# A hybrid decoder block: the output projection by seven block products in place of eight

## The chip, the cores and the metric

The kernel runs on one core of a Trainium2 chip. The metric is the device time of one execution in microseconds (us), the median of several runs; lower is better.

## The reference, cut to what matters

One decoder block works on 1024 tokens of width 2048 (with 16 learned tokens ahead of them): a normalisation, an input projection, eight heads of differential attention and a gated linear recurrence (RG-LRU) beside them. Their gated results stand side by side in `mixed`, 1024 features each. Then

```python
mixed = jnp.concatenate([att, rec], axis=-1)
x = x + jnp.einsum('bte,ed->btd', mixed, w_out[l])
return rmsnorm(x, final_g, NORM_EPS)[:, N_META:]
```

The change touches this last part alone: a product of 1024 x 2048 (tokens by features) with 2048 x 2048 (`w_out`), the residual, and the final normalisation, all in float32. `rmsnorm` divides a row by the root of the mean of its squares, so it needs a whole row of the output before it can scale any of it, and multiplies by `final_g`.

## The kernel before, in words

Four kinds of engine take part: TensorE (PE; its weight loads are PEld) multiplies, VectorE (DVE), ScalarE (ACT) and GpSimd (POOL) work element by element. DMAs are issued from SyncE's queue (SP) and from POOL's. Every queue is worked off in order. The code says what is computed; a scheduler sets the order of each queue ahead of time, and `issue_after` ties an instruction behind another one. A tile of a pool with `bufs=n` waits until the n-th tile of its tag before it is free.

Each float32 operand is split into a high part, rounded to the format that TensorE multiplies in, and a low part, the rest (`split`, lines 77 to 80: ScalarE copies `hi`, VectorE subtracts `lo`). A product is three matmuls into one accumulator: high by high, high by low, low by high (lines 643 to 645).

The tokens are worked in two halves of 512 (A and B). The mixed features of half h lie in DRAM as `mix_d[h][e]`, 16 tiles of 128 features by 512 tokens, 256 KB each; e 0 to 7 come from attention, 8 to 15 from the recurrence. `w_out` is stored as tiles `w_out[cg, ep]` of 128 x 1024 (512 KB): column group cg (512 output columns, four of them) and two blocks of 128 features, ep 0 to 7.

`load_w` (line 111) loads such a tile into `wraw` (two buffers) and splits it into `whi` and `wlo` (three buffers each). `load_mix` (line 611) loads and splits a tile of mix.

`out_half` (line 617) is run for half A, then for half B. Its loop goes over the four column groups; in each over eight weight tiles; for each of these over two feature blocks and four blocks of 128 tokens (t), so 24 matmuls of 512 columns to a weight tile. Four PSUM accumulators of a column group take 16 feature blocks each; eight buffers allow the next group to begin. While A is worked, its rows of x are loaded into `y` (four tiles of 128 x 2048) and, in column group 1, the 16 mix tiles of B into a second pool. At the end of a column group, `evacuate` adds each accumulator to `y` on VectorE (line 650), squares it on ScalarE with a running sum (line 651), and on POOL multiplies the first three column groups by `final_g` (line 653). After the fourth, `finish` works out the row's factor (lines 662 to 666), scales the row on ScalarE (L675) and VectorE (L671, L674) and stores it in two DMAs of 512 KB (L677), from POOL's queue for A, from SP's for B.

In the last column group of half B all eight weight tiles are split ahead of time into the buffers that held A's mix tiles (`wlast`), and the loop goes token block by token block, so that a block's end lies beside the matmuls of the next.

Before this stage, the recurrence of half B (lines 797 to 809) uses `hTB` on the right-hand side of SBUF and its own pool on the left.

Of the kernel before, what the change touches and what calls it, by code (L numbers as in the profile page):

```python
# [66 lines left out]
class Trunk:  # L67
# [549 lines left out]
    def out_half(self, half, mix, ypool, next_pool, next_mix, w_pool):  # L617

        nc = self.nc
        ys = []  # L620

        def load_y(t):
            y = ypool.tile([P, D], F32, tag="y", name="y", bufs=4)
            r = half * HALF + t * P
# [4 lines left out]
        def weights(cg, ep):
            if cg < 3 or w_pool is None:  # L630
                (hi, lo), = self.load_w(lambda i: self.w_out[cg, ep], 0, 1)
            else:
                raw = self.wpool.tile([P, 1024], F32, tag="wraw", name="wraw", bufs=2)
                nc.sync.dma_start(out=raw, in_=self.w_out[cg, ep])
                hi, lo = [w_pool.tile([P, 2, HALF], F32R, tag="mix", name="wlast", bufs=16).rearrange("p a b -> p (a b)")
                          for _ in range(2)]
                self.split(hi, lo, raw)
            return [(hi[:, i * 512:(i + 1) * 512], lo[:, i * 512:(i + 1) * 512]) for i in range(2)]

        def product(acc, e, t, w):  # L640
            tk = slice(t * P, (t + 1) * P)
            mh, ml = mix[e][:, 0, tk], mix[e][:, 1, tk]
            nc.tensor.matmul(acc, lhsT=mh, rhs=w[0], start=(e == 0), stop=False)  # L643
            nc.tensor.matmul(acc, lhsT=mh, rhs=w[1], start=False, stop=False)  # L644
            nc.tensor.matmul(acc, lhsT=ml, rhs=w[0], start=False, stop=(e == 15))  # L645

        def evacuate(acc, cg, t):
            y, ss = ys[t]
            c = slice(cg * 512, (cg + 1) * 512)
            nc.vector.tensor_tensor(out=y[:, c], in0=acc, in1=y[:, c], op=ALU.add)  # L650
            nc.scalar.activation(acc, y[:, c], AF.Square, accum_out=ss[:, cg:cg + 1])
            if cg < 3:
                nc.gpsimd.tensor_tensor(out=y[:, c], in0=y[:, c], in1=self.g_b[:, c], op=ALU.mult)
            if cg == 2:
                nc.vector.tensor_reduce(out=ss[:, 4:5], in_=ss[:, 0:3], axis=AX.X, op=ALU.add)
                nc.vector.tensor_scalar(out=ss[:, 4:5], in0=ss[:, 4:5], scalar1=1.0 / D, scalar2=EPS,
                                        op0=ALU.mult, op1=ALU.add)

        def finish(t):
            y, ss = ys[t]  # L660
            r, v, n, m = ss[:, 5:6], ss[:, 3:4], ss[:, 6:7], ss[:, 7:8]
            nc.scalar.activation(r, v, AF.Sqrt, bias=ss[:, 4:5], scale=1.0 / D)
            nc.vector.tensor_scalar(out=v, in0=v, scalar1=1.0 / D, scalar2=ss[:, 4:5], op0=ALU.mult, op1=ALU.add)
# [4 lines left out]
            for q in range(2):  # L668
                c = [slice(1024 * q + 512 * i, 1024 * q + 512 * (i + 1)) for i in range(2)]
# [9 lines left out]
        for cg in range(4):  # L679
            acc = [self.ps.tile([P, 512], F32, tag="o", name="o", bufs=8) for _ in range(4)]  # L680
            if cg == 3 and w_pool is not None:
                ws = sum([weights(cg, ep) for ep in range(8)], [])
                for t in range(4):
                    for e in range(16):
                        product(acc[t], e, t, ws[e])
                    evacuate(acc[t], cg, t)
                    finish(t)
                continue
            for ep in range(8):
                ws = weights(cg, ep)  # L690
                with self.tc.issue_after(self.last_w.ins):
                    if cg == 0 and 3 <= ep < 7:
                        load_y(ep - 3)
                    if cg == 0 and ep == 2 and not half:
                        nc.sync.dma_start(out=self.g_b, in_=self.final_g.partition_broadcast(P))
                        nc.vector.tensor_scalar(out=self.g_b, in0=self.g_b, scalar1=-0.5, scalar2=None, op0=ALU.mult)
                    if cg == 1 and not half:
                        for _ in range(2):
                            next_mix.append(self.load_mix(next_pool, 1, len(next_mix)))
                for i in range(2):  # L700
                    for t in range(4):
                        product(acc[t], 2 * ep + i, t, ws[i])
            for t in range(4):
                evacuate(acc[t], cg, t)
                if cg == 3:
                    finish(t)

    def build(self):
# [11 lines left out]
        self.vm_d = [dram.tile([MR, P], F32, name=f"vm_d{h}") for h in range(H)]  # L720
        self.mix_d = [[dram.tile([P, HALF], F32, name=f"mix_d{x}_{e}") for e in range(16)] for x in range(2)]
# [148 lines left out]
```

## Time and profile before

| | us |
|---|---|
| median of 3 runs | 1667.31 |
| lowest and highest run | 1664.11, 1668.2 |
| the profiled execution, its own time | 1665.55 |
| span of that execution in the trace | 1663.8 |

The profile is a page and a trace of one execution. The page gives the busy time of each engine, the span in 40 slices, and the chain of work that ended last, followed back from the last instruction. The trace can be asked for groups of instructions (by line, engine and tile, with their mean duration and what ended the idle time before them), for an engine's instructions in order of time, for busy time in any stretch, and for the DMAs with their time from issue to landing. A matmul's busy time overlaps that of its neighbours, so its price is the distance between two of them and not its duration. `fg_b` is the tile that holds `final_g`, `o` an accumulator of the output projection.

### The profile page before, as it was taken

How to read it: one execution, taken by the hardware profiler on the slowest of the kernel's cores; microseconds unless marked ns; L12 is line 12 of the kernel's file. 1: busy time of each engine (PE TensorE's matmuls, PEld its weight loads, DVE VectorE, ACT ScalarE, POOL GpSimd, SP SyncE). 2: the span in 40 equal slices, each digit the busy share in tenths (PEclk: the TensorE clock that was granted, in tenths of full speed). 3: DMA queues.
4: the chain of work that ended last, by engine and by line, in shares of the span. 5: the costliest groups of instructions: out<-in, count | busy, mean ns of one | idle time of the engine just before them, and what ended most of it. 6: DMA issues, size and time to landing. Idle time of an engine off the chain costs nothing.

```text
span 1663.8 us, 22995 instructions
## 1 busy us (share of the span) xinstructions
PE 1635.2 (98%) x8658; PEld 1404.3 (84%) x8658; DVE 1013.0 (61%) x2090; ACT 863.5 (52%) x1368; POOL 173.4 (10%) x276
## 2 busy tenths in 40 slices
PE   8999999999999999999999999999999999999997
PEld 6889988999988898888888888887878888888886
DVE  7766556665667667667766866776776553343342
ACT  5655455554475575546555655655875442232232
POOL 1211101111011102001101100000000011111110
PEclk9999999999999999999999999999999999999999
DMA  9633334433344435424323423314433462345332
GB/s 313 200 123 122 112 120 135 132 115 121 112 146 156 131 136 198 116 87 131 124 85 118 130 79 118 107 62 133 143 120 114 179 244 98 99 172 221 101 127 101
DMA packets 68427, 223.85 MB, mean 135 GB/s; under 512 B 9739, under 2 KB 11828, under 8 KB 67164
## 3 DMA queue, kind: packets, MB, share of 16 engines
q1 hardware_dynamic: 46720, 164.91, 29.6%
q0 software_dynamic: 21360, 57.41, 10.9%
q8 instruction: 68, 1.11, 0.3%
q14 instruction: 43, 0.35, 0.1%
q10 hardware_dynamic: 236, 0.06, 0.0%
HBM read 186.09 MB, written 29.37 MB: 130 GB/s over the span
## 4 chain that ended last, share of the span: by engine, by line
PE 89%; issue 3%; DVE 3%; DMA 3%; ACT 2%; POOL 0%; SPq 0%; ACTq 0%; POOLq 0%; DVEq 0%
PE proj L158 19%; PE proj L159 19%; PE proj L160 19%; PE o L645 7%; PE o L644 7%; PE o L643 7%; PE T L396 2%; PE S L341 2%; PE S L339 2%; PE pv L406 1%; PE pv L405 1%; PE pv L407 1%; DMA xraw<-xa 1%; DMA xt<-x 1%; DMA wraw<-w_in 1%
## 5 line engine op out<-in xcount | busy, mean ns | idle before, releaser
L80 DVE TENSOR_TENSOR wlo<-wraw,whi 128x1024 fp32r<-128x1024 f32 (+1 forms) x250 | 307.4, 1230 | 261.8 <-ACT whi L79 261.5
L79 ACT ACTIVATE whi<-wraw 128x1024 fp32r<-128x1024 f32 (+1 forms) x250 | 262.2, 1049 | 384.2 <-PE proj L159 187.0
L158 PE MATMUL proj<-hTA,whi 128*128 128x256 f32 (+2 forms) x1152 | 373.0, 325 | 0.8 <-ACT whi L79 0.7
L159 PE MATMUL proj<-hTA,whi 128*128 128x256 f32 (+2 forms) x1152 | 369.8, 322 | 0.0
L160 PE MATMUL proj<-hTA,wlo 128*128 128x256 f32 (+2 forms) x1152 | 369.2, 321 | 0.5 <-DVE wlo L80 0.5
L158 PE MATMUL proj<-hTB,whi 128*128 128x512 f32 x768 | 302.0, 393 | 1.2 <-DVE gr L291 0.6
L160 PE MATMUL proj<-hTB,wlo 128*128 128x512 f32 x768 | 300.9, 392 | 0.0
L159 PE MATMUL proj<-hTB,whi 128*128 128x512 f32 x768 | 299.7, 390 | 0.0
L158 PEld LDWEIGHTS proj<-hTA,whi 128*128 128x128 f32 x1152 | 218.3, 190 | 17.5 <-ACT whi L79 1.5
L160 PEld LDWEIGHTS proj<-hTA,wlo 128*128 128x128 f32 x1152 | 218.2, 190 | 16.3 <-DVE wlo L80 0.7
L159 PEld LDWEIGHTS proj<-hTA,whi 128*128 128x128 f32 x1152 | 218.6, 190 | 14.3
L644 PE MATMUL o<-wlo,mix 128*128 128x512 f32 x448 | 174.3, 389 | 0.0
L645 PE MATMUL o<-whi,mix 128*128 128x512 f32 x448 | 174.3, 389 | 0.0
L643 PE MATMUL o<-whi,mix 128*128 128x512 f32 x448 | 173.9, 389 | 0.0
L158 PEld LDWEIGHTS proj<-hTB,whi 128*128 128x128 f32 x768 | 144.3, 188 | 30.4 <-DVE gr L291 2.6
L160 PEld LDWEIGHTS proj<-hTB,wlo 128*128 128x128 f32 x768 | 144.2, 188 | 30.1
L159 PEld LDWEIGHTS proj<-hTB,whi 128*128 128x128 f32 x768 | 144.3, 188 | 28.5
L358 ACT ACTIVATE s<-s,st 128x144 f32<-128x144 f32 (+7 forms) x128 | 99.9, 782 | 50.9 <-DVE st L356 50.1
L643 PEld LDWEIGHTS o<-whi,mix 128*128 128x128 f32 x448 | 84.1, 188 | 17.8 <-ACT gate L488 0.3
L644 PEld LDWEIGHTS o<-wlo,mix 128*128 128x128 f32 x448 | 84.1, 188 | 17.5
L645 PEld LDWEIGHTS o<-whi,mix 128*128 128x128 f32 x448 | 84.1, 188 | 17.3
L351 DVE TENSOR_SCALAR_CACHE_REDUCE s<-S,b 128x256 f32<-128x256 f32 (+5 forms) x176 | 82.8, 478 | 19.4 <-PE S L341 16.2
(227 smaller groups left out, 2175.3 us busy)
## 6 DMA issues: line engine op xcount, KB each, us to landing
wraw<-w_in SPq DMA_DIRECT2D x190, 512.0 KB, 3.9
wraw<-w_out SPq DMA_DIRECT2D x64, 512.0 KB, 3.5
mix<-mix_d SPq DMA_DIRECT2D x32, 256.0 KB, 4.3
y<-x SPq DMA_DIRECT2D x8, 1024.0 KB, 10.1
kk_d<-kk POOLq DMA_DIRECT2D x8, 528.0 KB, 3.0
kk<-kk_d POOLq DMA_DIRECT2D x8, 528.0 KB, 4.2
xt<-x SPq DMA_DIRECT2D x8, 512.0 KB, 10.6
qq<-qf POOLq DMA_DIRECT2D x32, 128.0 KB, 3.7
```

The source lines that it names most:

```text
L79: nc.scalar.activation(hi, src, AF.Copy)
L80: nc.vector.tensor_tensor(out=lo, in0=src, in1=hi.bitcast(F32), op=ALU.subtract)
L158: nc.tensor.matmul(ps[:, :n], lhsT=hi[:, c], rhs=xh, start=(kt == 0), stop=False)
L159: nc.tensor.matmul(ps[:, :n], lhsT=hi[:, c], rhs=xl, start=False, stop=False)
L160: nc.tensor.matmul(ps[:, :n], lhsT=lo[:, c], rhs=xh, start=False, stop=(kt == KT - 1))
L339: nc.tensor.matmul(ps[:, :w], lhsT=qq[:, j, qc], rhs=kk[:, j, c0:c0 + w], start=True, stop=False)
L341: nc.tensor.matmul(ps[:, :w], lhsT=self.qz[:, j, qc], rhs=kl[:, c0:c0 + w], start=False, stop=True)
L351: nc.vector.tensor_scalar(out=s[j][:, a:a + n], in0=ps[:, a - c0:a - c0 + n], scalar1=self.b31[:, h:h + 1], scalar2=-3.0e38, op0=ALU.add, ...
L358: nc.scalar.activation(s[j][:, :s_len], s[j][:, :s_len], AF.Exp, bias=nm[:, j:j + 1], accum_out=l[:, j:j + 1])
L643: nc.tensor.matmul(acc, lhsT=mh, rhs=w[0], start=(e == 0), stop=False)
L644: nc.tensor.matmul(acc, lhsT=mh, rhs=w[1], start=False, stop=False)
L645: nc.tensor.matmul(acc, lhsT=ml, rhs=w[0], start=False, stop=(e == 15))
```

## The change

The output projection is written as a product of 2 x 2 blocks. The rows of X are the token halves A and B, its columns the feature halves (e 0 to 7, and 8 to 15); `w_out` is cut by feature halves and, for each pair of column groups, into a left column group (cg 0 or 2) and a right one (cg 1 or 3). Eight block products become seven (Winograd's form of Strassen's scheme), with sums and differences of blocks as factors:

S1 = X21 + X22, S2 = S1 - X11, S3 = X11 - X21, S4 = X12 - S2 on the left; T1 = W12 - W11, T2 = W22 - T1, T3 = W22 - W12, T4 = T2 - W21 on the right.

- `out_proj` takes the place of both calls of `out_half`. Its outer loop is the list `plan` of seven products, X11 W11, X12 W21, S1 T1, S4 W22, S2 T2, S3 T3 and X22 T4; in each it goes over both column pairs, four weight tiles each, and the same 24 matmuls to a tile. An accumulator takes 8 feature blocks, not 16.
- `right_factor` loads a weight tile; for T1 to T4 it loads a second one into a new tile `wb` (three buffers), subtracts on VectorE, and for T1 and T2 stores the result to DRAM (`t1_d`, `t2_d`) from POOL's queue, to be read again by T2 and T4. Then it splits as before.
- `left_factor` makes the left factor of the next product, one tile of 512 tokens in each step: loads from `mix_d` into a mix buffer and new tiles `xb` (four buffers), adds or subtracts on VectorE, splits. With S1 it works out S2, too, and stores it to DRAM (`s2_d`) from POOL's queue. So 40 mix-sized tiles are made in this stage (before, 16 were loaded).
- All output rows stay in SBUF: `ys`, eight tiles of 128 x 2048 on the right-hand side (where `hTB` was). Loads of x go into them during products 1 and 2, by columns, apart from the left column groups of the lower half, where product 1 is copied by ScalarE and x is added at the end on POOL, from a tile of its own.
- `sink` adds an accumulator to one or two places (`add`, `sub`, `left`, `copy`, `x`). When a column group of a row is final, the square and the multiplication by `final_g` follow as before; after a row's fourth, `finish`. The upper half's rows end at product 5, the lower half's at product 7.
- In product 7, second pair, the four weight tiles are split ahead of time into mix buffers, and the loop goes token block by token block.

The diff, cut to its core:

```diff
+    def left_factor(self, name, pool, stage, e):
...
+        src = {"s1": (B[e], B[8 + e]), "s4": (A[8 + e], self.s2_d[e]), "s2": (self.s2_d[e], None),
+               "s3": (A[e], B[e]), "x22": (B[8 + e], None)}[name]
+        t = pool.tile([P, 2, HALF], F32R, tag="mix", name="mix", bufs=16)
+        x = t[:, 1].bitcast(F32)
+        nc.sync.dma_start(out=x, in_=src[0])
+        if src[1] is not None:
+            b = stage.tile([P, HALF], F32, tag="xb", name="xb", bufs=4)
+            nc.sync.dma_start(out=b, in_=src[1])
+            nc.vector.tensor_tensor(out=b, in0=x, in1=b, op=ALU.add if name == "s1" else ALU.subtract)
+            x = b
+        if name == "s1":
+            b = stage.tile([P, HALF], F32, tag="xb", name="xb", bufs=4)
+            nc.sync.dma_start(out=b, in_=A[e])
+            nc.vector.tensor_tensor(out=b, in0=x, in1=b, op=ALU.subtract)
+            nc.gpsimd.dma_start(out=self.s2_d[e], in_=b)
+        self.split(t[:, 0], t[:, 1], x)
+        return t
+
+    def right_factor(self, name, pair, ep, stage, home):
...
+        src = {"w11": (w(1, 1), None, None), "w21": (w(2, 1), None, None), "w22": (w(2, 2), None, None),
+               "t1": (w(1, 2), w(1, 1), t1), "t2": (w(2, 2), t1, t2), "t3": (w(2, 2), w(1, 2), None),
+               "t4": (t2, w(2, 1), None)}[name]
+        raw = self.wpool.tile([P, 1024], F32, tag="wraw", name="wraw", bufs=2)
+        self.last_w = nc.sync.dma_start(out=raw, in_=src[0])
+        if src[1] is not None:
+            b = stage.tile([P, 1024], F32, tag="wb", name="wb", bufs=3)
+            self.last_w = nc.sync.dma_start(out=b, in_=src[1])
+            nc.vector.tensor_tensor(out=b, in0=raw, in1=b, op=ALU.subtract)
+            raw = b
+        if src[2] is not None:
+            nc.gpsimd.dma_start(out=src[2], in_=raw)
...
+        self.split(hi, lo, raw)
...
+    def out_proj(self, mix, xpool, stage, ypool):
...
+        def sink(kind, acc, half, t, cg, final):
+
+            y, s = ys[half][t], ss[half][t]
+            c = slice(cg * 512, (cg + 1) * 512)
+            if kind == "copy":
+                nc.scalar.activation(y[:, c], acc, AF.Copy)
+            elif kind == "x":
+                b = stage.tile([P, HALF], F32, tag="xb", name="xr", bufs=4)
+                nc.sync.dma_start(out=b, in_=self.x[half * HALF + t * P:half * HALF + (t + 1) * P, c])
+                nc.gpsimd.tensor_tensor(out=y[:, c], in0=y[:, c], in1=b, op=ALU.add)
             else:
...
+                other = ys[1][t][:, (cg & 2) * 512:(cg & 2) * 512 + 512] if kind == "left" else acc
+                nc.vector.tensor_tensor(out=y[:, c], in0=y[:, c], in1=other, op=ALU.subtract if kind == "sub" else ALU.add)
+            if not final:
+                return
...
+            if n == 3:
+                finish(half, t, cg)
...
+        plan = [("w11", None, [("add", 0, 0, 0), ("copy", 1, 0, 0)]),
+                ("w21", "s1", [("add", 0, 0, 1)]),
+                ("t1", "s4", [("add", 0, 1, 0), ("add", 1, 1, 0)]),
+                ("w22", "s2", [("add", 0, 1, 0)]),
+                ("t2", "s3", [("add", 1, 0, 0), ("left", 0, 1, 1)]),
+                ("t3", "x22", [("add", 1, 0, 0), ("left", 1, 1, 1), ("x", 1, 0, 0)]),
+                ("t4", None, [("sub", 1, 0, 1)])]
+        x, x_next = mix[:8], mix[8:]
+        for k, (right, left, sinks) in enumerate(plan):
+            ahead = []
+            for pair in range(2):
+                acc = [self.ps.tile([P, 512], F32, tag="o", name="o", bufs=8) for _ in range(4)]
...
+                if k == 6 and pair == 1:
+                    ws = sum([self.right_factor(right, pair, ep, stage, xpool) for ep in range(4)], [])
+                    for t in range(4):
+                        for e in range(8):
+                            product(acc[t], x[e], t, ws[e], e == 0, e == 7)
+                        evacuate(t)
+                    continue
+                for ep in range(4):
+                    ws = self.right_factor(right, pair, ep, stage, None)
+                    with self.tc.issue_after(self.last_w.ins):
+                        if k < 2:
+                            load_y(pair, k, ep)
...
+                        if left:
+                            ahead.append(self.left_factor(left, xpool, stage, 4 * pair + ep))
+                    for i in range(2):
+                        for t in range(4):
+                            e = 2 * ep + i
+                            product(acc[t], x[e], t, ws[i], e == 0, e == 7)
                 for t in range(4):
...
+                    evacuate(t)
+            x, x_next = (x_next, None) if k == 0 else (ahead, None)
...
-        yp = fin.enter_context(tc.tile_pool(name="yp", bufs=1, side="left", reuse_waits="tile"))
-        m2 = fin.enter_context(tc.tile_pool(name="m2", bufs=1, side="right", reuse_waits="tile"))
...
-        self.out_half(0, mixA, yp, m2, mixB, None)
-        m2.tile([P, self.pad_right], F32, name="pad_m")
-        self.out_half(1, mixB, yp, None, None, m1)
+        stage = fin.enter_context(tc.tile_pool(name="stage", bufs=1, side="left", reuse_waits="tile"))
+        yp = fin.enter_context(tc.tile_pool(name="yp", bufs=1, side="right", reuse_waits="tile"))
+        self.g_b = stage.tile([P, D], F32, name="fg_b")
+        self.out_proj(mixA, m1, stage, yp)
```

## Rows read from the trace of the kernel before

**Rows 1.** The page: busy time, VectorE in 40 slices, the chain.

```profile
PE 1635.2 (98%) x8658; PEld 1404.3 (84%) x8658; DVE 1013.0 (61%) x2090; ACT 863.5 (52%) x1368; POOL 173.4 (10%) x276
...
DVE  7766556665667667667766866776776553343342
...
PE 89%; issue 3%; DVE 3%; DMA 3%; ACT 2%; POOL 0%; SPq 0%; ACTq 0%; POOLq 0%; DVEq 0%
```

**Rows 2.** Output stage, `o` tiles alone: PE, PEld, DVE, ACT, clock, DMA.

```profile
1306.70:1655.20 348.50, 348.44 (x1536) 288.20 (x1536) 20.77 (x32) 21.40 (x62) 1.00 0.43 152
```

**Rows 3.** Same stretch, all tiles: PE, PEld, DVE, ACT, POOL, clock, DMA, GB/s.

```profile
1306.70:1655.20 348.50, 348.44 (x1537) 288.20 (x1536) 132.82 (x176) 111.67 (x169) 41.98 (x33) 1.00 0.43 152
```

**Rows 4.** Groups by shape, output stage: busy us, mean ns | idle before.

```profile
L80 DVE TENSOR_TENSOR wlo<-wraw,whi 128x1024 fp32r<-128x1024 f32 x54 | 70.1, 1297 | 155.0 <-ACT whi L79 154.9
L79 ACT ACTIVATE whi<-wraw 128x1024 fp32r<-128x1024 f32 x54 | 57.2, 1059 | 162.3 <-PE o L645 119.4 <-DMA wraw<-w_out 30.3 <-issue 12.6
...
L650 DVE TENSOR_TENSOR y<-o,y 128x512 f32<-128x512 f32 x32 | 21.4, 689 | 27.4 <-PE o L645 27.4
L651 ACT ACTIVATE o<-y 128x512 f32<-128x512 f32 x32 | 18.9, 592 | 44.4 <-DVE y L650 44.4
...
L675 ACT ACTIVATE y<-y,ss 128x512 f32<-128x512 f32 x16 | 10.6, 712 | 3.4 <-DVE ss L666 3.4
...
L671 DVE SCALAR_TENSOR_TENSOR y<-y,ss,fg_b 128x512 f32<-128x512 f32 x8 | 6.0, 747 | 0.0
...
L674 DVE TENSOR_SCALAR y<-y,ss 128x512 f32<-128x512 f32 x8 | 3.9, 483 | 0.4
...
L663 DVE TENSOR_SCALAR ss<-ss 128x1 f32<-128x1 f32 x8 | 1.7, 209 | 4.6 <-ACT ss L662 4.5
```

**Rows 5.** VectorE in time order: start, duration, line, instruction, idle before it.

```profile
1351.11 2.48 DVE L650 TENSOR_TENSOR y<-o,y 128x512 f32<-128x512 f32 x4
1354.14 2.12 DVE L80 TENSOR_TENSOR wlo<-wraw,whi 128x1024 fp32r<-128x1024 f32 x1 [0.56 <-ACT whi L79]
1356.19 3.48 DVE L80 TENSOR_TENSOR mix<-mix 128x512 fp32r<-128x512 f32 x2
...
1361.24 1.32 DVE L80 TENSOR_TENSOR mix<-mix 128x512 fp32r<-128x512 f32 x2 [0.43 <-ACT mix L79]
1362.82 1.22 DVE L80 TENSOR_TENSOR wlo<-wraw,whi 128x1024 fp32r<-128x1024 f32 x1 [0.26 <-ACT whi L79]
```

**Rows 6.** GpSimd in order of time, the same stretch.

```profile
1352.63 6.49 POOL L653 TENSOR_TENSOR y<-y,fg_b 128x512 f32<-128x512 f32 x4 [35.08 <-DMA mix<-mix_d]
```

**Rows 7.** Busy time by stretch: PE, PEld, DVE, ACT, POOL; clock, DMA share, GB/s.

```profile
14.00:20.00 6.00, 6.00 (x41) 5.46 (x40) 5.89 (x10) 3.23 (x4) 0.00 (x0) 1.00 0.86 282
1318.00:1336.00 18.00, 18.00 (x81) 14.92 (x80) 4.79 (x4) 3.08 (x3) 0.00 (x0) 1.00 0.97 391
1480.00:1490.00 10.00, 10.00 (x46) 8.29 (x45) 9.80 (x29) 9.84 (x22) 3.33 (x7) 1.00 0.60 227
1484.00:1512.00 28.00, 28.00 (x126) 23.17 (x125) 10.20 (x24) 10.32 (x15) 4.31 (x8) 1.00 0.98 379
```

**Rows 8.** DMA issues of the output stage: count, KB each, median us to landing.

```profile
wraw<-w_out SPq DMA_DIRECT2D x60, 512.0 KB, 3.5
```

**Rows 9.** DMA issues from 1484 to 1512 us, loads and stores.

```profile
out<-y POOLq DMA_DIRECT2D x8, 512.0 KB, 7.0
...
wraw<-w_out SPq DMA_DIRECT2D x4, 512.0 KB, 6.1
```

**Rows 10.** DMA issues from 1318 to 1336 us, loads alone.

```profile
y<-x SPq DMA_DIRECT2D x4, 1024.0 KB, 11.0
wraw<-w_out SPq DMA_DIRECT2D x3, 512.0 KB, 11.3
```

**Rows 11.** One row's end in the last column group, in order of time.

```profile
1644.30 0.69 DVE L650 TENSOR_TENSOR y<-o,y 128x512 f32<-128x512 f32 x1 [7.08 <-PE o L645]
...
1647.35 0.75 DVE L671 SCALAR_TENSOR_TENSOR y<-y,ss,fg_b 128x512 f32<-128x512 f32 x1
```

More of the change, by code (lines that the diff above doesn't have):

```diff
@@ new lines, in left_factor @@
+        A, B = self.mix_d
+        src = {"s1": (B[e], B[8 + e]), "s4": (A[8 + e], self.s2_d[e]), "s2": (self.s2_d[e], None),
[8 more added lines that the diff above has]
+            x = b
@@ new lines, in left_factor @@
+        if name == "s1":
[6 more added lines that the diff above has]
+    def right_factor(self, name, pair, ep, stage, home):
+        nc = self.nc
+        w = lambda r, c: self.w_out[2 * pair + c - 1, 4 * (r - 1) + ep]
+        t1, t2 = self.t1_d[pair][ep], self.t2_d[pair][ep]
+        src = {"w11": (w(1, 1), None, None), "w21": (w(2, 1), None, None), "w22": (w(2, 2), None, None),
[10 more added lines that the diff above has]
+            nc.gpsimd.dma_start(out=src[2], in_=raw)
+        if home is None:
+            hi = self.wpool.tile([P, 1024], F32R, tag="whi", name="whi", bufs=3)
+            lo = self.wpool.tile([P, 1024], F32R, tag="wlo", name="wlo", bufs=3)
+        else:
+            hi, lo = [home.tile([P, 2, HALF], F32R, tag="mix", name="wlast", bufs=16).rearrange("p a b -> p (a b)")
+                      for _ in range(2)]
+        self.split(hi, lo, raw)
+        return [(hi[:, i * 512:(i + 1) * 512], lo[:, i * 512:(i + 1) * 512]) for i in range(2)]
@@ new lines, in out_proj, with load_y, product @@
+    def out_proj(self, mix, xpool, stage, ypool):
+        nc = self.nc
+        ys = [[ypool.tile([P, D], F32, name=f"y{half}_{t}") for t in range(4)] for half in range(2)]
+        ss = [[stage.tile([P, 8], F32, name=f"ss{half}_{t}") for t in range(4)] for half in range(2)]
+        done = {}
+        def load_y(pair, half, t):
+            c = slice(1024 * pair + 512 * half, 1024 * pair + 1024)
+            r = half * HALF + t * P
+            nc.sync.dma_start(out=ys[half][t][:, c], in_=self.x[r:r + P, c])
+        def product(acc, x, t, w, start, stop):
+            tk = slice(t * P, (t + 1) * P)
+            nc.tensor.matmul(acc, lhsT=x[:, 0, tk], rhs=w[0], start=start, stop=False)
+            nc.tensor.matmul(acc, lhsT=x[:, 0, tk], rhs=w[1], start=False, stop=False)
+            nc.tensor.matmul(acc, lhsT=x[:, 1, tk], rhs=w[0], start=False, stop=stop)
+        def sink(kind, acc, half, t, cg, final):
[7 more added lines that the diff above has]
+                nc.gpsimd.tensor_tensor(out=y[:, c], in0=y[:, c], in1=b, op=ALU.add)
+            else:
+                other = ys[1][t][:, (cg & 2) * 512:(cg & 2) * 512 + 512] if kind == "left" else acc
+                nc.vector.tensor_tensor(out=y[:, c], in0=y[:, c], in1=other, op=ALU.subtract if kind == "sub" else ALU.add)
+            if not final:
+                return
+            n = done[half, t] = done.get((half, t), -1) + 1
+            nc.scalar.activation(acc, y[:, c], AF.Square, accum_out=s[:, n:n + 1])
+            if n < 3:
@@ L668, in finish @@
             for q in range(2):
-                c = [slice(1024 * q + 512 * i, 1024 * q + 512 * (i + 1)) for i in range(2)]
+                c = [slice(512 * cg, 512 * cg + 512) for cg in ((2, 3) if last == 3 else (3, 2))] if q else \
+                    [slice(0, 512), slice(512, 1024)]
                 if q:
@@ L677, in finish @@
                 (nc.sync if half else nc.gpsimd).dma_start(out=self.out[row, c], in_=y[:, c])
[L679 to L682, printed above, removed]
-                for t in range(4):
[L684 to L706, printed above, removed]
@@ new lines, in tiles @@
+        def tiles():
+            return [self.ps.tile([P, 512], F32, tag="o", name="o", bufs=8) for _ in range(4)]
+        plan = [("w11", None, [("add", 0, 0, 0), ("copy", 1, 0, 0)]),
[5 more added lines that the diff above has]
+                ("t4", None, [("sub", 1, 0, 1)])]
```

55 lines of the change are left out of this document (17 added, 38 removed).

## Prediction

> **What bounds the kernel now.** I read the engine shares and the chain of work that ended last first [rows 1]: TensorE (PE) is busy 98% of the span and holds 89% of the chain, so a matmul taken away is time taken away, as long as the others keep pace. Then the output projection by itself. Its 1536 matmuls stand from 1306.7 to 1655.2 us, 348.5 us, and PE is busy for 348.44 of it [rows 2]: there is no gap to win there, and the granted clock is 1.00, the upper level of 2.4 GHz. One matmul thus costs 348.5 / 1536 = 0.2269 us (the 389 ns that the matmul groups show overlap their neighbours). In the same stretch VectorE (DVE) is busy 132.82 us, 38% [rows 3], and the DMA engines 0.43 of the time. So DVE and the transfers are hidden now; the question is whether they still are.
>
> I count in **steps**: one weight tile of 128x1024 and its 24 matmuls, 24 x 0.2269 = 5.446 us. Before there are 64 steps, after there are 7 products x 2 column pairs x 4 = 56. A product is 8 steps, 43.56 us; a half-product (one pair) is 21.78 us.
>
> **What it removes.** 8 steps, 192 matmuls: 43.56 us, if every later step still takes 5.446 us. The rest of the text asks what the other steps cost beyond that.
>
> **DVE, step by step.** Prices: a 128x1024 subtraction 1.23 us (the group's mean is 1.297 [rows 4], an undisturbed one 1.22 [rows 5]); a 128x512 subtraction or addition 0.69 (L650); the end of a row of output (L663 and three as small, L674, L671) 4 x 0.21 + 0.48 + 0.75 = 2.07 us [rows 4]. Before, a step has one 128x1024 split and little else. After:
> - products 3 and 5 (t1 with s4, t2 with s3): combine and split the weights, 2 x 1.23, combine and split the left factor, 2 x 0.69: 3.84 us a step.
> - product 6 (t3 with x22): 2.46 + 0.69 = 3.15. Product 7 (t4): 2.46. Product 2 (w21 with s1): 1.23 + 3 x 0.69 = 3.3. Product 4 (w22 with s2): 1.92. Product 1: 1.23.
> - the sinks of a half-product: four tiles at 0.69 for one addition each (2.8), 1.38 for two (5.5). They are run during the half-product after it.
> - GpSimd (POOL). Four POOL multiplications took 6.49 us in one stretch [rows 6], and in it one weight split took 2.12 us for 1.22 and two mix splits 3.48 for 1.32 [rows 5]: 3.06 us lost, 0.77 us of DVE for each POOL operation. The change keeps the 24 multiplications (8 row blocks by 3 column groups) and adds 8 additions (the residual of the lower half, the "x" sink).
>
> Most half-products fit into 21.78 us: the third product needs 15.4 + 2.8 + 3.1 = 21.3 and 15.4 + 5.5 = 20.9. From the second half of product 5 on they don't:
> - product 5, pair 1: 15.4 + sinks of pair 0 with the two small sums 4 x (1.38 + 0.42) = 7.2 + four POOL operations 3.1 = 25.7
> - product 6, pair 0: 12.6 + 5.5 + four row ends 8.3 = 26.4
> - product 6, pair 1: 12.6 + 5.5 + eight POOL operations 6.1 = 24.2
> - product 7, pair 0: 9.8, the last four weight tiles, which must be ready at its end, 9.8, 5.5, and 6.1 = 31.2
>
> Together 107.5 us against 4 x 21.78 = 87.1, 20.4 too much. Against that stands the lead: three whi/wlo buffers let DVE be two steps ahead at the start (2 x 3.84 = 7.7 us), and the last weight tile may come 18 matmuls (4.1 us) into the last half-product. So 20.4 - 11.8 = 8.6 us of PE waiting, if DVE never idles. That is one end; below it the end is 0, since back to back operations overlap a little (four L650 in 2.48 us, 0.62 each, not 0.69 [rows 5]). The other end: in no fortieth of the span is DVE 80% busy [rows 1]; at 80% the work takes 134.4 us, 47.3 - 11.8 = 35.5 us lost. Where it had a backlog it was busy 9.80 of 10 us [rows 7], so I take a value near the first end, **12 us**.
>
> **The transfers.** Bytes of a product, by 512 KB weight tiles and 256 KB halves: product 3 reads two tiles and two halves a step and writes one tile, 2048 KB, 16.78 MB in all; product 5 the same; product 6 reads two tiles and a half a step, eight halves of x and sends out four rows of 1 MB, 16.78 MB too; product 2 moves 14.68 MB; the others at most three quarters of that. So three products need 16.78 MB / 43.56 us = 385 GB/s. Loads of y, weights and final_g together reached 391 GB/s over 18 us with PE undisturbed, loads and stores mixed 379 over 28 us [rows 7]. So the transfers sit at the edge, and I add **3 us** for them (0 at 391; at 379 it is 44.3 - 43.56 = 0.7 us a product, and they stay full for longer than any row shows). The Trainium skill's page "DMA: Bandwidth & Descriptors", section Specifications, puts the HBM limit of a core at about 358 GB/s, which speaks against this change: 46.9 us a product, 10 us in all instead of 3, and 1646 us by the sum below. The 391 GB/s measured with nearly all of it read from HBM doesn't agree with that limit for a core that runs alone.
>
> **What I cost at nothing, and its cover.** ScalarE: in product 6, pair 0, four weight splits at 1.06, four half-size ones, four squares at 0.59 with read-out and the row ends with two 0.71 each [rows 4] stay under 17 us of 21.78. SyncE's queue: a load of y now goes behind the first weight tile and waits for the last LRU projection, whose SBUF it takes over; the next weight tile stands behind it. At 3.5 us to land [rows 8] and 2.3 us to split it is ready about when the first step (5.4 us) ends; without that cover it costs up to a step, once. The POOL queue gets 24 stores (s2, t1, t2); s2's buffer is busy for a load, two operations and a store, at saturated landings 6.1 + 1.4 + 7.0 us [rows 9], 14.5 against two steps (10.9), but at light ones well below; it concerns product 2 alone, where the rate is lower, bound 0 to 14 us, taken as 0. The accumulators: eight PSUM buffers, so a sink may be 21 us late. The row ends: each row of the last half-product has 5.4 us, and its chain on DVE took 3.8 us (1644.30 to 1648.10) [rows 11]; what follows the last matmul stays 1663.8 - 1655.2 = 8.6 us.
>
> **Sum.** The profiled execution took 1665.55 us (span 1663.8), 1.8 below the median of the runs. 1665.55 - 43.56 + 12 + 3 = 1637.0, with the 1.8 **1639 us**.
>
> **Rivals.**
> - A, nothing is lost: DVE works ahead further than I count. Then 1667.3 - 43.6 = 1624 (up to 1628). For it: PE never waited in this stage, even when the window was full. Against it: 107.5 us of work in 87.1. Chance 0.20.
> - B, the transfers set the pace in products 2, 3, 5 and 6. Early in the kernel the engines moved 282 GB/s at 0.86 busy [rows 7], 328 if full; the new 256 KB halves have rows of 2 KB, half of a weight tile's. At 328, products 3, 5, 6 take 51.2 us each and product 2 44.8: 22.8 + 1.2 = 24 lost; with up to 12 of DVE's on top 1648 to 1660. Against it: 379 and 391. Chance 0.18.
> - C, slower than before or level: the two wraw buffers. Where weights are combined, each is held from its load's issue until the subtraction has read it, and every later load stands behind that on SyncE's queue. A step then can't be shorter than half of that turn. With the landing of 11.3 us that weight tiles had behind four loads of y [rows 10], plus 1.23, plus one other split ahead of it, 13.8 us: 6.9 us a step, 1.45 too long in 32 steps (products 3, 5, 6, 7), 46 us: 1670. It decides from a landing of 11.2 us on; at 6.1 us [rows 9] the turn is 8.6, inside two steps. For it: three products run the DMA engines near their full rate, as in [rows 10]. Against it: there 4 MB stood ahead, here some 2 MB. Chance 0.20, of which 0.06 fall within 0.3% of 1667.3 and 0.14 above.
> - My forecast, DVE late from product 5 on, 1628 to 1650: chance 0.42.
>
> **Numbers.** Faster by over 0.3% (about what a measurement of this kernel can tell from no change): 0.20 + 0.18 + 0.42 = 0.80; same 0.06; slower 0.14. The range takes in A with the run spread, 1622, and reaches up through B to 1667, which leaves out C's slower part and little else.
>
> **What would show it.** Right: 1344 matmuls in the stage; PE gaps that gather in products 5 to 7 and end on wlo or whi (DVE, ScalarE), with DVE above 90% busy there and the first four products at 43.6 us each; the DMA share near 1.0 in products 3, 5, 6. A: no gaps, stage 305 us. B: gaps in product 2 or 3 already, with DVE waiting on DMA landings and a rate below 350 GB/s. C: SyncE waiting for the subtraction on wraw, weight tiles landing after 11 us or more. The forecast is wrong if the stage's steps stretch in products 1 or 4, or if matmuls themselves get slower than 0.227 us apart.

## The result, and the profile after

The changed kernel takes 1639.57 us (median of 4 runs, 1637.0 to 1642.84) against 1667.76 for the kernel before (4 runs beside it). The ratio is 0.9836, with a 95% interval of 0.9812 to 0.986: 28 us or 1.6% faster. The forecast was 1639, the range 1622 to 1667. The total agrees, by luck: of the terms that made it, one was right and the others weren't, and that is what this part is about.

The page of the changed kernel, the rows that answer to [rows 1]:

```profile
PE 1596.9 (98%) x8466; PEld 1370.8 (84%) x8466; DVE 1117.6 (68%) x2218; ACT 874.1 (53%) x1392; POOL 205.2 (13%) x308
...
DVE  6766556665676667667668667757877656867996
...
PE 75%; DVE 8%; issue 7%; DMA 7%; ACT 3%; POOL 1%; SPq 0%; ACTq 0%; DVEq 0%; POOLq 0%
```

PE is as busy as before, but its share of the chain fell from 89% to 75%, and VectorE's slices in the stage, 2 to 5 before, are 5 to 9 now. The stage is no longer PE's alone.

I cut the stage at the first matmul of each half-product. These are the fourteen half-products in order, two to a product, with the columns of [rows 7] (length; PE, PEld, DVE, ACT, POOL busy; clock, DMA share, GB/s):

```profile
1308.33:1330.22 21.89, 21.89 (x98) 18.13 (x97) 11.26 (x13) 10.23 (x12) 0.54 (x1) 1.00 0.80 296
1330.22:1351.98 21.76, 21.76 (x98) 18.02 (x96) 11.34 (x14) 7.57 (x10) 1.08 (x2) 1.00 0.86 299
1351.98:1373.74 21.76, 21.76 (x98) 18.02 (x96) 13.31 (x19) 7.56 (x12) 1.64 (x3) 1.00 0.87 313
1373.74:1398.35 24.61, 22.42 (x98) 17.86 (x96) 17.81 (x20) 8.77 (x16) 9.14 (x8) 1.00 0.82 265
1398.35:1425.65 27.30, 23.96 (x98) 19.04 (x97) 22.29 (x24) 9.89 (x17) 9.49 (x9) 0.94 0.98 343
1425.65:1447.41 21.76, 21.76 (x98) 18.02 (x97) 16.46 (x22) 6.56 (x8) 1.07 (x2) 1.00 0.95 360
1447.41:1469.17 21.76, 21.76 (x98) 18.02 (x97) 13.43 (x18) 7.31 (x9) 0.00 (x0) 1.00 0.48 161
1469.17:1490.93 21.76, 21.76 (x98) 18.02 (x97) 14.24 (x17) 6.78 (x8) 1.60 (x3) 1.00 0.75 249
1490.93:1512.69 21.76, 21.76 (x98) 18.02 (x97) 17.10 (x22) 6.44 (x8) 2.13 (x4) 1.00 1.00 388
1512.69:1534.45 21.76, 21.76 (x98) 18.02 (x97) 20.97 (x29) 9.36 (x16) 7.09 (x5) 1.00 0.92 335
1534.45:1556.21 21.76, 21.76 (x98) 18.02 (x97) 21.76 (x44) 15.33 (x28) 4.22 (x8) 1.00 0.83 282
1556.21:1577.97 21.76, 21.76 (x98) 18.02 (x97) 19.18 (x16) 7.14 (x13) 15.07 (x9) 1.00 0.94 360
1577.97:1602.42 24.45, 22.05 (x98) 17.95 (x96) 24.00 (x18) 7.56 (x13) 15.29 (x9) 1.00 0.57 184
1602.42:1626.30 23.88, 22.12 (x97) 17.75 (x95) 15.04 (x37) 11.77 (x25) 5.05 (x4) 1.00 0.31 123
```

All 1344 matmuls are there (the 97s and 98s are matmuls that reach over an edge). Ten of the fourteen take 21.8 us, the price forecast from [rows 2]: in order of time, 24 matmuls of a step lie 5.44 us apart here as before. So 56 steps make 304.6 us, and the stage, from 1308.33 to 1626.30, took 318.0: 13.3 us are lost, of the 43.56 that the product left out gives. Where: 2.85 us in the second half of product 2, 5.54 in the first half of product 3, and 4.79 in product 7. Products 5 and 6, where I had put the first of VectorE's lateness, lose nothing, although VectorE is busy for 20.97, 21.76 and 19.18 of three half-products. The spans differ by 1663.8 - 1635.2 = 28.6 us: the stage is 348.5 - 318.0 = 30.5 shorter, it began 1.6 us later, and after the last matmul stand 8.9 us, not 8.6.

What PE waited for in the stage (time in total, times, the longest):

```profile
PE o L685 <- DVE wlo L80: 7.9, 5, 2.4
PE o L685 <- DVE wlast L80: 1.8, 1, 1.8
```

It is always a low part of the weights, VectorE's last operation on them. These six waits are 9.7 of the 13.3 us; 1.6 more went to a lower clock (last section). That says who was late, not why. The rows of product 7's first half show one why. First VectorE (start, duration, instruction), then GpSimd, in order of time:

```profile
1578.42 1.23 DVE L80 TENSOR_TENSOR wlo<-wb,whi 128x1024 fp32r<-128x1024 f32 x1 [1.21 <-ACT whi L79]
1579.56 1.22 DVE L658 TENSOR_TENSOR wb<-wraw,wb 128x1024 f32<-128x1024 f32 x1
1580.69 1.28 DVE L700 TENSOR_TENSOR y<-y,o 128x512 f32<-128x512 f32 x2
1581.89 0.68 DVE L700 TENSOR_TENSOR y<-y 128x512 f32<-128x512 f32 x1
1582.49 0.68 DVE L700 TENSOR_TENSOR y<-y,o 128x512 f32<-128x512 f32 x1
1583.09 1.40 DVE L700 TENSOR_TENSOR y<-y 128x512 f32<-128x512 f32 x1
1584.42 0.67 DVE L700 TENSOR_TENSOR y<-y,o 128x512 f32<-128x512 f32 x1
1585.02 1.40 DVE L700 TENSOR_TENSOR y<-y 128x512 f32<-128x512 f32 x1
1586.34 2.31 DVE L80 TENSOR_TENSOR wlo<-wb,whi 128x1024 fp32r<-128x1024 f32 x1
1588.57 2.31 DVE L658 TENSOR_TENSOR wb<-wraw,wb 128x1024 f32<-128x1024 f32 x1
```

```profile
1582.65 1.29 POOL L697 TENSOR_TENSOR y<-y,xr 128x512 f32<-128x512 f32 x1 [4.28 <-DVE y L700]
1584.57 1.29 POOL L697 TENSOR_TENSOR y<-y,xr 128x512 f32<-128x512 f32 x1 [0.63 <-DVE y L700]
1585.82 3.98 POOL L706 TENSOR_TENSOR y<-y,fg_b 128x512 f32<-128x512 f32 x2
1589.76 2.27 POOL L697 TENSOR_TENSOR y<-y,xr 128x512 f32<-128x512 f32 x1
```

Until 1583 a 128x512 operation takes 0.68 us and the next one begins 0.60 later, a 128x1024 operation 1.22. Beside GpSimd's additions (from 1582.65 on, and without a pause from 1585.82) they take 1.40 and 2.31, and GpSimd's own then take 2.27 in place of 1.29: each waits for the other in turn. Only operations with both inputs in SBUF are stretched. `y<-y,o`, with one input in PSUM, keeps 0.67 at 1584.42, in the midst of it.

The other why is in products 2 and 3. SyncE's queue and VectorE at the end of product 2:

```profile
1375.86 0.33 SPq L654 DMA_DIRECT2D wraw<-w_out  x1
1376.24 0.51 SPq L680 DMA_DIRECT2D y<-x  x1
1376.84 0.44 SPq L631 DMA_DIRECT2D mix<-mix_d  x1
1377.33 0.43 SPq L634 DMA_DIRECT2D xb<-mix_d  x1
...
1386.09 0.33 SPq L654 DMA_DIRECT2D wraw<-w_out  x1
```

```profile
1374.60 1.23 DVE L80 TENSOR_TENSOR wlo<-wraw,whi 128x1024 fp32r<-128x1024 f32 x1 [0.26 <-ACT whi L79]
1379.99 0.69 DVE L635 TENSOR_TENSOR xb<-mix,xb 128x512 f32<-128x512 f32 x1 [4.16 <-DMA xb<-mix_d]
...
1384.85 1.22 DVE L80 TENSOR_TENSOR wlo<-wraw,whi 128x1024 fp32r<-128x1024 f32 x1
```

A weight split ends at 1375.83, which frees its raw buffer; only then, at 1375.86, SyncE issues the next raw tile, and behind it in its queue the loads of y, mix and xb, the last at 1377.33. VectorE's next instruction in order needs that xb tile, and stands idle for 4.16 us, with other work behind it. Its next weight split comes at 1384.85, after seven other operations (four of them sinks), and the raw load after that at 1386.09. The two queues, each in order, wait for each other in a ring: split, raw load, xb load behind it, sum, split. Over the stretch from 1352 to 1425 us, SyncE's longest two groups of waits and VectorE's:

```profile
SPq L654 <- DVE wlo L80: 14.6, 6, 6.1
SPq L639 <- DMA s_d<-xb: 7.3, 4, 3.5
```

```profile
DVE xb L635 <- DMA xb<-mix_d: 13.8, 4, 5.1
```

I called this theory R (the two raw buffers, with the fixed orders). Against it stood X (the four xb tiles, held by s2's stores: the 7.3 us above) and B (the transfer rate). For product 7, theory P (GpSimd shuts VectorE out) stood against D (VectorE has too much work of its own).

### The profile page after: what moved, and what is told of

The parts are those of the page before. It is cut to its first block, busy times and chain, and to the rows that moved or that the text cites. A ratio compares the mean times of both kernels' runs of the same rounds, so it can differ in the third digit from the quotient of the medians.

```text
span 1635.2 us, 22985 instructions
## 1 busy us (share of the span) xinstructions
PE 1596.9 (98%) x8466; PEld 1370.8 (84%) x8466; DVE 1117.6 (68%) x2218; ACT 874.1 (53%) x1392; POOL 205.2 (13%) x308
## 4 chain that ended last, share of the span: by engine, by line
PE 75%; DVE 8%; issue 7%; DMA 7%; ACT 3%; POOL 1%; SPq 0%; ACTq 0%; DVEq 0%; POOLq 0%
PE proj L158 20%; PE proj L159 19%; PE proj L160 19%; PE T L396 2%; PE o L685 2%; PE o L686 2%; PE o L684 2%; DVE wlo L80 2%; PE S L341 2%; PE S L339 2%; DMA wb<-w_out 1%; DVE y L700 1%; DVE wb L658 1%; DMA xb<-mix_d 1%; DMA xt<-x 1%
## 5 line engine op out<-in xcount | busy, mean ns | idle before, releaser
L79 ACT ACTIVATE whi<-wraw 128x1024 fp32r<-128x1024 f32 (+1 forms) x218 | 228.2, 1047 | 244.8 <-PE proj L159 186.6
L80 DVE TENSOR_TENSOR wlo<-wraw,whi 128x1024 fp32r<-128x1024 f32 (+1 forms) x218 | 264.0, 1212 | 116.5 <-ACT whi L79 116.3
L685 PE MATMUL o<-wlo,mix 128*128 128x512 f32 x416 | 163.2, 392 | 7.9 <-DVE wlo L80 7.9
L159 PEld LDWEIGHTS proj<-hTB,whi 128*128 128x128 f32 x768 | 144.3, 188 | 28.6
L686 PE MATMUL o<-whi,mix 128*128 128x512 f32 x416 | 162.6, 391 | 0.0
L684 PE MATMUL o<-whi,mix 128*128 128x512 f32 x416 | 162.5, 391 | 0.0
L685 PEld LDWEIGHTS o<-wlo,mix 128*128 128x128 f32 x416 | 78.4, 189 | 26.4 <-DVE wlo L80 10.0
L684 PEld LDWEIGHTS o<-whi,mix 128*128 128x128 f32 x416 | 78.5, 189 | 16.6 <-ACT gate L488 0.3
L686 PEld LDWEIGHTS o<-whi,mix 128*128 128x128 f32 x416 | 78.5, 189 | 16.2
```

Of the source, the lines that this page charges most:

```text
L79: nc.scalar.activation(hi, src, AF.Copy)
L80: nc.vector.tensor_tensor(out=lo, in0=src, in1=hi.bitcast(F32), op=ALU.subtract)
L159: nc.tensor.matmul(ps[:, :n], lhsT=hi[:, c], rhs=xl, start=False, stop=False)
L684: nc.tensor.matmul(acc, lhsT=x[:, 0, tk], rhs=w[0], start=start, stop=False)
L685: nc.tensor.matmul(acc, lhsT=x[:, 0, tk], rhs=w[1], start=False, stop=False)
L686: nc.tensor.matmul(acc, lhsT=x[:, 1, tk], rhs=w[0], start=False, stop=stop)
```

## The experiments

Ten kernels, each the changed kernel with the edit shown; one profiled run of each, and five timed ones of e7_both. Stage: first to last matmul. Lost: what the steps of a product took beyond 5.44 us each, from the starts of the matmuls in order of time (all 1344 are in every trace). The times are single runs but for two, and the changed kernel's own four lie 5.8 us apart, so the stage is the column to read.

| | stage | lost in product 1 | 2 and 3 | 5 and 6 | 7 | time |
|---|---|---|---|---|---|---|
| the changed kernel | 318.0 | 0.1 | 8.4 | 0.0 | 4.8 | 1639.57 (median) |
| e10_same, once more | 317.3 | 0.1 | 5.1 | 0.0 | 7.4 | 1636.58 |
| e1_xb8 | 320.4 | 0.1 | 6.3 | 1.1 | 8.3 | 1640.68 |
| e2_raw3 | 320.7 | 5.2 | 0.3 | 5.8 | 4.8 | 1641.65 |
| e3_no_y2 | 311.3 | 0.1 | 0.1 | 0.0 | 6.5 | 1631.89 |
| e4_no_pool6 | 313.0 | 0.1 | 5.7 | 2.6 | 0.0 | 1632.71 |
| e5_dve | 311.0 | 0.1 | 6.2 | 0.0 | 0.0 | 1631.33 |
| e6_raw3_late | 314.3 | 0.1 | 0.0 | 6.5 | 3.1 | 1631.65 |
| e7_both | 306.1 | 0.1 | 0.0 | 1.3 | 0.0 | 1625.49 (median) |
| e8_y2_act | 317.1 | 0.1 | 4.1 | 0.0 | 8.2 | 1635.71 |
| e9_wb5 | 311.9 | 0.1 | 4.8 | 0.0 | 2.4 | 1631.66 |

**The changed kernel itself again**, with no edit; the others are read by it:

> The changed kernel itself once more, for the spread of where it loses time: 12 to 15 us lost in the stage, of which 6 to 9 in products 2 and 3 and 4 to 7 in product 7, nothing in products 1, 4 and 5 beyond 0.5. If the places move, the single-look comparisons of the other experiments count only where they differ by more than the two looks at this kernel do.

The total is as expected, 12.7 us, but the split isn't: 5.1 and 7.4 against 8.4 and 4.8. Of the 3.3 us between 8.4 and 5.1, 1.6 are the lower clock in product 3, which this trace doesn't have. So in a column only differences above 3 us or so count.

**More xb tiles.**

```diff
-            b = stage.tile([P, HALF], F32, tag="xb", name="xb", bufs=4)
+            b = stage.tile([P, HALF], F32, tag="xb", name="xb", bufs=8)
```

> Eight xb buffers in place of four, nothing else. In the changed kernel the stage lasts 318.0 us from its first matmul to its last, 13.3 more than 56 steps of 5.44 us: 8.4 us at the end of product 2 and the start of product 3, 4.8 in product 7. Theory X (the xb tiles' turn, with the store of s2 in it, holds SyncE's queue in product 2): the loss in products 2 and 3 falls from 8.4 to 3 us or less, product 7 keeps its 4.8, the stage takes 311 to 313 us. Theory R (the two wraw buffers and the fixed order of VectorE set it): the 8.4 stays within 2 us. Theory B (the transfer rate sets it): it stays as well.

6.3 us lost in products 2 and 3, between the 5.1 and 8.4 of the kernel without the edit. X, which wanted 3 or less, falls: SyncE no longer waits for the stores of s2 from 1352 to 1425 us (7.3 before), and the loss stays.

**A third raw buffer.**

```diff
-        raw = self.wpool.tile([P, 1024], F32, tag="wraw", name="wraw", bufs=2)
+        self.turn = getattr(self, "turn", -1) + 1
+        raw = stage.tile([P, 1024], F32, tag="wr3", name="wr3", bufs=1) if self.turn % 3 == 2 else \
+            self.wpool.tile([P, 1024], F32, tag="wraw", name="wraw", bufs=2)
```

> A third buffer for the raw weight tiles of this stage (every third tile in a new one), nothing else. Theory R: SyncE can issue a step earlier, VectorE no longer waits for xb landings that were issued late, and the loss in products 2 and 3 falls from 8.4 to 3 us or less; in product 7 it falls too, by 1 to 2 us, since the last weight tiles come earlier. Theory X: 8.4 stays within 2 us, since the stall on s2's stores remains. Theory B: it stays or grows, since more loads are in flight at once.

Products 2 and 3 lose 0.3 us, as R said, with all their bytes. But the run is no faster: product 1 lost 5.2, since the new buffer lies where the recurrence's tiles were, and the load of it held SyncE's queue until they were free (8.1 us for its last product, `sg`), and product 6 lost 5.5, a point taken up below. Product 7 lost 4.8, 1.6 of it by the lower clock; R had wanted 1 to 2 us less there than before.

**The same bytes less 2 MB in product 2.**

```diff
-                        if k < 2:
+                        if k < 1:
                             load_y(pair, k, ep)
+                            nc.vector.memset(ys[1][ep][:, 1024 * pair + 512:1024 * pair + 1024], 0.0)
```

> Product 2 loads no x: the eight loads of 256 KB for the right column groups of the lower half are replaced by a fill with zeros on VectorE in product 1 (the residual of that quarter of the output is left out). Product 2's bytes fall from 14.7 to 12.6 MB, 290 GB/s at full pace. Theory B: the loss in products 2 and 3 falls from 8.4 to 4 us or less. Theories X and R: each loses an issue of 0.4 us a step on SyncE's queue and some landing time, so the loss falls by 1 to 3 us only.

The loss there is gone, 0.1 us. I had expected that of B alone and 1 to 3 us less by R, so taken by itself this speaks for B. What decides against B are the rates at which nothing was lost: 388 GB/s over 21.76 us in product 5 of the changed kernel, in the table above, more than the 343 at which product 3 lost 5.5; and the third buffer, which took the loss away with the bytes unchanged. Fewer loads in the ring (one in five on SyncE's queue) would let it turn faster, too; that this is why the loss went is not shown.

**Product 6 without GpSimd.**

```diff
             elif kind == "x":
+                return
...
-            if n < 3:
+            if n < 3 and not (half == 1 and n < 2):
```

> Product 6's sinks without GpSimd: the additions of x to the left column groups of the lower half (with their loads) and the multiplications of its right column groups by final_g are left out, 16 GpSimd operations. Theory P (GpSimd shuts VectorE out, which doubles VectorE's operations in the first half of product 7): VectorE's 128x1024 operations there go back from 2.3 to 1.2 us, and product 7's loss from 4.8 to 0.5 us or less; products 2 and 3 keep 8.4. Theory D (VectorE has too much work of its own there): the durations stay above 2 us or the loss stays above 3 us.

Product 7's loss goes from 4.8 (7.4 in its second trace) to 0.0, and its VectorE operations to their short durations. The same place in this kernel:

```profile
1585.94 1.22 DVE L658 TENSOR_TENSOR wb<-wraw,wb 128x1024 f32<-128x1024 f32 x1
1587.08 0.69 DVE L701 TENSOR_TENSOR y<-y 128x512 f32<-128x512 f32 x1
1587.68 1.22 DVE L80 TENSOR_TENSOR wlo<-wb,whi 128x1024 fp32r<-128x1024 f32 x1
```

The groups of the whole stage show it at one line: the additions of `y` to `y` (L700 in the changed kernel, L701 here), same shape, same count, mean 1272 and 689 ns. First the changed kernel (with the additions of accumulators, which keep 680 ns), then this one:

```profile
L700 DVE TENSOR_TENSOR y<-y,o 128x512 f32<-128x512 f32 x64 | 41.1, 680 | 4.4 <-PE o L686 4.4
...
L700 DVE TENSOR_TENSOR y<-y 128x512 f32<-128x512 f32 x8 | 9.9, 1272 | 0.0
```

```profile
L701 DVE TENSOR_TENSOR y<-y 128x512 f32<-128x512 f32 x8 | 5.5, 689 | 0.0
```

The 2.6 us that products 5 and 6 lose here were not expected and aren't explained, and this kernel leaves out eight loads along with GpSimd's work. The next one leaves out nothing.

**GpSimd's work on VectorE**, the same test without leaving anything out:

```diff
-                nc.gpsimd.tensor_tensor(out=y[:, c], in0=y[:, c], in1=b, op=ALU.add)
+                nc.vector.tensor_tensor(out=y[:, c], in0=y[:, c], in1=b, op=ALU.add)
...
-                nc.gpsimd.tensor_tensor(out=y[:, c], in0=y[:, c], in1=self.g_b[:, c], op=ALU.mult)
+                nc.vector.tensor_tensor(out=y[:, c], in0=y[:, c], in1=self.g_b[:, c], op=ALU.mult)
```

> The 32 element-wise operations of GpSimd in this stage (24 multiplications by final_g, 8 additions of x) go to VectorE; GpSimd only issues stores. Theory P (an operation of GpSimd that reads SBUF shuts VectorE out for its whole time, so the two engines share one lane here): VectorE gets 32 operations of some 0.65 us, but none of its others is stretched; the loss in product 7 falls from 4.8 us to 1 or less, in products 2 and 3 it stays at 5 to 9, the stage takes 311 to 314 us. Theory D (VectorE's own work is the limit in products 6 and 7): 21 us more of it make the loss there 8 us or more.

Product 7 loses nothing, with 32 operations more on VectorE in the stage. D falls, P stands: GpSimd's operations cost VectorE more time than doing them there. Products 2 and 3 keep their loss (6.2), as expected. So GpSimd isn't needed for that one, though in the changed kernel it stretches VectorE there, too: from 1385.98 to 1391.09 us three 128x512 operations take 1.77, 1.68 and 1.78 us.

**The third raw buffer from product 2 on** (the diff is against e2_raw3).

```diff
-        raw = stage.tile([P, 1024], F32, tag="wr3", name="wr3", bufs=1) if self.turn % 3 == 2 else \
+        raw = stage.tile([P, 1024], F32, tag="wr3", name="wr3", bufs=1) if self.turn >= 8 and self.turn % 3 == 2 else \
```

> The third raw buffer again, but used from product 2 on only, so that product 1 doesn't wait for its place in SBUF. Theory R: products 2 and 3 lose 1 us or less, as with the third buffer before (0.8), product 1 loses 0.5 or less (6.3 before). Products 6 and 7 together lose 5 to 9 us, since GpSimd's operations are still there. Stage 311 to 315 us. If the gain in products 2 and 3 came from the delay in product 1 instead (a later start that let the loads run ahead), they lose 5 us or more again.

Product 1 is free of loss and products 2 and 3 lose nothing, so the gain there was the buffer's, not the delay's. Their two halves in which the changed kernel loses time, the second of product 2 and the first of product 3 (columns as above):

```profile
1371.99:1393.75 21.76, 21.76 (x97) 18.02 (x96) 17.77 (x19) 8.03 (x15) 10.19 (x9) 1.00 0.92 335
1393.75:1415.51 21.76, 21.76 (x97) 18.03 (x96) 19.36 (x21) 8.97 (x16) 9.06 (x7) 1.00 0.90 314
```

The bytes are the same, and the raw tiles land no sooner: after 6.7 us (the new buffer's) and 7.1 us (the others) in the median of these two halves, against 6.5 in the changed kernel's. One thing is not separated: with the edit the scheduler also put SyncE's loads into another order (e9 below suggests that order counts). All three kernels with the third buffer lose 0.3 us or less in products 2 and 3; of the others, only the one with fewer loads does.

Products 5 to 7 lose 9.5. In this kernel PE reaches product 6 9.7 us earlier than in the changed one, and now waits there. The next one shows how much of that is GpSimd's.

**Both**, the edits of e5_dve and e6_raw3_late.

> Both: the third raw buffer from product 2 on, and GpSimd's element-wise work on VectorE. By theories R and P the two losses are separate and both go: stage 306 to 309 us, the run 1627 to 1631 us, some 9 us below the changed kernel's 1639.6. If one of them only moves the wait to the other place, the stage stays above 312 us.

1625.49 us (median of 5 runs, 1622.47 to 1626.56), ratio to the kernel before 0.9746, interval 0.9729 to 0.9763: below both kernels, since the changed one's interval begins at 0.9812. The stage takes 306.1 us, 1.5 more than its steps; the gain over the changed kernel is 14 us by the medians, not the 9 that I expected (the stage, as expected, gives 11.9 of it; the rest is spread between runs). PE's waits in the stage, and VectorE's from 1352 to 1425 us:

```profile
PE o L687 <- DVE wlo L80: 1.0, 1, 1.0
```

```profile
DVE xb L635 <- DMA xb<-mix_d: 2.9, 1, 2.9
```

The 13.8 us that VectorE had idled for xb tiles are 2.9.

**Loads of x from another queue.**

```diff
-            nc.sync.dma_start(out=ys[half][t][:, c], in_=self.x[r:r + P, c])
+            (nc.scalar if half else nc.sync).dma_start(out=ys[half][t][:, c], in_=self.x[r:r + P, c])
```

> Product 2's eight loads of x are issued from ScalarE's queue, not from SyncE's; the same bytes. Theory R in its narrow form (what stands ahead of an xb load on SyncE's queue makes it late): the loss in products 2 and 3 falls from 8.4 us to 4 or less. If the landing times are what counts (more bytes in flight), it stays within 2 us of 8.4, as it does not with the loads left out (0.1).

4.1 us against 8.4 and 5.1: inconclusive, by the spread of those two.

**More wb tiles.**

```diff
-            b = stage.tile([P, 1024], F32, tag="wb", name="wb", bufs=3)
+            b = stage.tile([P, 1024], F32, tag="wb", name="wb", bufs=5)
```

> Five wb buffers in place of three, nothing else: a tile that holds T1 or T2 is free again only when its store to DRAM has landed, and SyncE waited 13.1 us in product 3 for that. If that wait makes the 5.5 us lost in product 3, they fall to 2 or less. Theory R (two raw buffers, with which SyncE's queue can't issue early enough) expects product 3 to keep 4 us or more, since the queue waits for the subtraction that frees the raw buffer instead. Product 2 keeps 1 to 3 us either way.

SyncE's wait for the stores in product 3 fell from 13.1 to 5.2 us, its wait for the subtraction rose from 9.2 to 13.7, and product 3 keeps 4.8 us (1.6 of it the lower clock, as in the changed kernel), so the stores of t1 aren't its cause, as R said. Product 2's loss went to 0.0, which no theory had; the order of SyncE's queue came out different in this build (the load of A that waits for s2's store now stands behind the next raw tile and not ahead of it), which fits the ring, but I ran nothing to show it. Product 7 lost 2.4 us, less than the 4.8 and 7.4 of the changed kernel, which no theory had either.

## Why the prediction was right, and where it wasn't

- **What it removes, 43.56 us: right.** 1344 matmuls, 5.44 us a step, and no matmul slower except eight at the lower clock (1.6 us in all, below).
- **VectorE, 12 us from product 5 on: the term was mis-sized, and its place wrong.** Measured 4.8 and 7.4 us in two traces, all in product 7. I counted 107.5 us of work in four half-products where the busy times are 20.97, 21.76, 19.18 and 24.00, 85.9 in all (a part of the last weight tiles came after). My price was an operation's duration, 0.69 and 1.23; back to back they follow each other every 0.60 and 1.14 us, as the rows from 1578 to 1583 show. With these the four sums are about 98 to 100 us, 11 to 13 too much against the lead of 11.8: at most about 1 us lost by VectorE's own work. I had seen four L650 in 2.48 us [rows 5] and used it for the lower bound alone. What is left is GpSimd. I had it right as a mechanism, 0.77 us for an operation [rows 5, 6]; in product 7 it was more like 1.1 (2.31 for 1.22, 1.40 or 1.78 for 0.68), and with it gone (e4, e5) the loss is gone. Over the 20 operations that I counted, 1.1 in place of 0.77 is 6.6 us, an estimate beside the 4.8 and 7.4. VectorE was busy for 88 to 100% of these four half-products, much as the prediction had it, yet products 5 and 6 lost nothing.
- **The transfers, 3 us: not there.** Product 5 ran at 388 GB/s in its first half and lost nothing. The Trainium skill's page "DMA: Bandwidth & Descriptors", section Specifications, gives about 358 GB/s of HBM bandwidth for a core, as half of what two cores share. Had that bound this core, which runs alone, the half-product would have waited; it didn't. Rival B with its 328 GB/s falls by the same row, although its signs were there: gaps in products 2 and 3, VectorE waiting for landings, 265 and 343 GB/s. A ring that turns slowly looks the same; e6, with the same bytes and no loss, tells them apart.
- **What I cost at nothing: here is the step that failed.** "SyncE's queue" and the bound of "0 to 14 us, taken as 0" for s2's buffer: 8.4 and 5.1 us in products 2 and 3 (1.6 of the 8.4 by the clock). e1 clears s2's buffer; what is left is SyncE's queue. I looked at each wait by itself and against the step, and each fits. The mechanism was rival C's, the raw buffer that holds every later load on the queue, which I had let decide only from a landing of 11.2 us on. Weight tiles landed after 4.3 us in the median of the stage, 6.5 from 1373 to 1426; by C's formula the turn is then 6.5 + 2 x 1.23 = 9.0 us, inside two steps. The turn was long for another reason: behind the raw load stood the xb load that VectorE needs before it gets to the split which frees the next raw buffer. I had one operation between landing and release; the queue had a second load, a landing and up to seven operations. In products 3 and 5 the same two buffers do without loss once the lead is back.
- **The rest:** 1.6 us at the stage's beginning and 0.3 at its end. The beginning lay between 1306.6 and 1310.2 us in the ten experiments, so that is spread.
- So 15 us were forecast lost and 13.3 were, by a sum whose parts were 12 + 3 + 0 and should have been about 5 + 0 + 8. That the total came out is luck: one part too large stood for one left out. Its own signs told of it: the first four products were to take 43.6 us each, and products 2 and 3 took 46.4 and 49.1. Rival A wasn't far in its substance: with both causes out, the stage loses 1.5 us (e7). A's number, 1624, is close to what e7 took, 1625.5.

What stays open: why the wait moves to product 6 when products 2 and 3 are mended alone (e2, e6: 5.5 and 6.1 us there). Without GpSimd's operations it is 1.3 (e7). In e6, PE's wait of 4.1 us there comes after VectorE has stood idle 2.9 us for a `wb` tile, before GpSimd begins; then GpSimd's operations stretch two of VectorE's by 1.8 us in all, ahead of the split that PE needs (1.39 and 1.75 for 0.68), and the lower clock adds 1.6. What makes the `wb` tile late there isn't shown.

## What to carry to other kernels

When one engine must never wait and another is busy for 60 to 100% of its time, as here, price each engine by the distance of its operations back to back, and then look not at single waits but for rings: a buffer that is freed by an operation which stands, in its queue's order, behind one that needs a load which stands, in the other queue's order, behind the load of that buffer. One buffer more broke it here. Element-wise work put on GpSimd to relieve VectorE does the opposite where both read two SBUF tiles: here 32 operations moved back to VectorE made the stage 6 to 7 us shorter.

## What the runs showed of the hardware

GpSimd and VectorE take turns, as the rows of product 7 show: 2.31 for 1.22 us on one, 2.27 for 1.29 on the other. The Trainium skill, on the page "SBUF — State Buffer", section "SBUF: two separate sides", calls it an exclusive lock that a VectorE operation with two SBUF inputs takes against a GpSimd operation that reads SBUF; the operations with a PSUM input, 0.68 us throughout, agree.

The clock did what I hadn't expected. After PE's wait at 1411 to 1413 us, the granted clock fell to 0.5, the lower of its two levels (1.2 of 2.4 GHz), some 1.5 us after PE had gone on, and was back between 1418 and 1420:

```profile
1408.00:1412.00 4.00, 3.40 (x16) 2.47 (x14) 4.00 (x6) 2.18 (x6) 1.97 (x2) 1.00 1.04 407
1412.00:1414.00 2.00, 0.74 (x3) 0.66 (x4) 2.00 (x2) 1.28 (x3) 2.00 (x2) 1.00 1.03 409
1414.00:1416.00 2.00, 2.00 (x8) 1.55 (x8) 2.00 (x2) 0.00 (x0) 2.00 (x2) 0.69 1.01 389
1416.00:1418.00 2.00, 2.00 (x6) 1.63 (x5) 2.00 (x3) 0.25 (x1) 0.62 (x2) 0.50 0.88 335
1418.00:1420.00 2.00, 2.00 (x10) 1.59 (x10) 2.00 (x3) 1.33 (x2) 0.01 (x1) 0.96 0.89 235
```

Eight matmuls stood 0.43 us apart in place of 0.227, and these 1.6 us are part of product 3's 5.54. A longer wait of the same run, 2.55 us at 1594, was followed by no such fall (1.00 throughout in slices of 2 us). In e5_dve the fall came as PE went on after a wait of 4 us. In eight of the eleven traces (not in e4, e7 and e10) some wait was followed by such a stretch of seven to nine slow matmuls, at 1.5 to 1.7 us each time. So a wait of 2.0 to 4.4 us here cost 1.6 us or so more, but not every time.
